# Token-major input and rope tables loaded ahead of the first product weights, and one Strassen sum made by VectorE

## The chip, the cores and the metric

The kernel runs on one core of a Trainium2 chip. The metric is the device time of one execution in microseconds (us), the median of several runs. The core has a matrix engine (TensorE, PE in the profile; its weight loads are PEld), a vector engine (VectorE, DVE), a scalar engine (ScalarE, ACT), a general engine (GpSimd, POOL) and a queue engine (SyncE, SP) that issues most of the transfers. Each takes its instructions in a fixed order that was decided when the program was built. Transfers (DMA) are issued from SP, ACT and POOL and run on 16 shared DMA engines.

## The reference, cut to what matters

Two layers over 512 tokens of width 1024, everything in float32. Each layer normalises its input, multiplies it by a wide input matrix whose columns are queries, keys, values and gates of two attention branches, runs both branches, and projects back.

```python
def rms_norm(x, w, eps):
    return xf * lax.rsqrt(jnp.mean(xf * xf, axis=-1, keepdims=True) + eps) * w

def hybrid_layer(x, layer, ...):
    hdn = rms_norm(x, norm_w, RMS_EPS)
    u = hdn @ w_in                       # 1024 x 10240
    qa, ka, va, za, qb, kb, vb, zb, ga, gb = split_cols(u)
    qa = partial_rope(qa, cos, sin)      # ka, qb, kb as well
    ya = dilated_mixture(qa, ka, va) * silu(za)
    ...                                  # yb: differential attention, silu(zb)
    merged = sigmoid(ga) * (ya @ w_proj_a) + sigmoid(gb) * (yb @ w_proj_b)
    return x + merged @ w_out
# two layers, then a final rms_norm
```

## The kernel before, in words

Every float32 product is made from three float32r products: each operand is split into a high part (a rounded copy) and a low part (the difference), and high x high, high x low and low x high are added up. The row scale of the norm is left out of the products; it is applied to their results. So the products of the first layer can begin before the norm is known, and only what reads their results waits for it.

The weights come as a stream of 512 KB pieces, numbered in the order of `plan()`: `raw0` and `raw1` are the first product chunk (z0, the first gate columns of branch A), `raw2` and `raw3` the second (z1), and eight entries, 4 to 11, the third, "v": the value columns of branch A, a kind "S" chunk. `load_to` (line 86) issues a piece from SP; the pieces of ordinary chunks have three buffers, those of S chunks come from a pool of 29 shared tiles (`blk`). `split` (line 100) makes `whi` (ScalarE, line 103) and `wlo` (VectorE, line 104), each with three buffers, so that a new `whi` waits until TensorE has done with the one three places back.

An S chunk is a 2 x 2 Strassen-Winograd product with seven block products instead of eight. Its weight operands are the quarters 11, 22, 21 and 12 (each in two pieces, p = 0 and 1) and the sums T1 = 12 - 11, T2 = T1 - 22, T3 = 12 - 22 and 21 + T2. `prep_S` (line 122) prepares the 14 operands in the order 11, 21, T1, T2, T3, 22, 21 + T2. T1 and T3 are made by `sum_of` (line 109): ScalarE writes the negative of 11 or 22 (line 112), and a transfer issued by POOL adds quarter 12 from memory to it (line 113, an accumulating transfer). T2 and 21 + T2 are made by VectorE (lines 135 and 137). In the order of TensorE, i.e. of `proj_S`, X takes 11, Z takes 21, Y takes T1, X takes T2, and so on; `S1` to `S4` are the sums on the other side (lines 213 to 238).

The norm's row scale of the first layer is made from a token-major copy of x, four pieces `xt0` to `xt3` (line 837): ScalarE squares and sums them (line 839, eight instructions), VectorE makes a mean (lines 248 and 240), POOL raises it to the power -1/2 (line 241), TensorE turns the result into rows (line 264, the tile `ps_rb`), ScalarE copies that to `rb` (line 269), and POOL multiplies the rope tables `ct` and `st` by it (lines 270 and 271). The evacuations of z0 and z1 on VectorE (line 467) wait for `rb`. `proj_T` (line 274) holds the results of z0 until all this is issued.

The order in each engine's queue is not the order of the code. A scheduler in the framework simulates the engines' times and puts the instructions into their queues by priority and by that simulation; only the first block of ScalarE and VectorE instructions (line 817) keeps its written order. So a change at the start may re-sort instructions elsewhere.

## Time and profile before

| | |
|---|---|
| median of 3 runs | 1385.66 us (1385.55 to 1386.77) |
| the profiled execution | 1387.04 us |
| its span, first to last instruction | 1385.3 us |
| mean granted TensorE clock | 0.994 of full speed |
| TensorE busy | 1351.1 us, 98% |
| VectorE busy | 969.4 us, 70% |
| ScalarE busy | 850.4 us, 61% |
| POOL busy | 324.2 us, 23% |
| moved by DMA | 205.04 MB, mean 148 GB/s |

Busy times are of instructions in flight; matrix products overlap each other, so a busy TensorE shows no idle time while a matrix product of 512 columns starts every 0.23 us. The span begins at the first instruction; the rest of the execution's own time (1.7 us) lies outside it. A gap of an engine is given in brackets in a timeline row, with what ended it.

### The profile page before, as it was taken

The page shows a single profiled execution, that of the slowest core. Times are in us where ns is not written, and L with a number is a line of the kernel's source. Part 1 is how long each engine was busy: PE and PEld are TensorE (multiplying, and loading weights), DVE is VectorE, ACT ScalarE, POOL GpSimd, SP SyncE. Part 2 cuts the span into 40 slices and gives each one's busy share as a digit, 9 for nine tenths or more (in the row PEclk, how much of TensorE's full clock was granted, in tenths as well). Part 3 has the DMA queues.
Part 4 walks back from the last instruction along what each step waited for, and adds up shares of the span by engine and source line. Part 5 has one row for each costly group of instructions (what it writes and reads, how often), then busy time and mean ns, then how long its engine had stood idle before and what let it go on. Part 6 is the DMA issues. An engine that isn't in the chain of part 4 may idle for free.

```text
span 1385.3 us, 19483 instructions
## 1 busy us (share of the span) xinstructions
PE 1351.1 (98%) x6712; PEld 1134.7 (82%) x6712; DVE 969.4 (70%) x1907; ACT 850.4 (61%) x1630; POOL 324.2 (23%) x453
## 2 busy tenths in 40 slices
PE   7799999999999999999999999999999999999996
PEld 6588888888888888888888888878888888888896
DVE  6666787788867786645485677788896678665553
ACT  6655678777555657632566567877756566664332
POOL 0210341333303241110220223232351223211000
PEclk9899999999999999999999999999999999999999
DMA  9654574555735454333586356554565464435231
GB/s 315 211 151 118 157 182 120 141 151 145 190 113 153 137 157 132 123 101 104 182 259 177 88 159 162 146 152 114 153 173 162 122 175 123 144 100 179 94 92 61
DMA packets 82594, 205.04 MB, mean 148 GB/s; under 512 B 11200, under 2 KB 27712, under 8 KB 82496
## 3 DMA queue, kind: packets, MB, share of 16 engines
q1 hardware_dynamic: 45888, 136.67, 30.8%
q0 software_dynamic: 19712, 58.74, 18.6%
q10 hardware_dynamic: 16896, 8.39, 2.0%
q8 instruction: 53, 0.87, 0.3%
q14 instruction: 45, 0.37, 0.1%
HBM read 136.65 MB, written 16.78 MB: 111 GB/s over the span
## 4 chain that ended last, share of the span: by engine, by line
PE 86%; DVE 6%; ACT 3%; DMA 2%; issue 1%; POOL 0%; SPq 0%; DVEq 0%; POOLq 0%; ACTq 0%
PE pj L288 20%; PE pj L289 20%; PE pj L290 20%; PE X L309 2%; PE X L311 2%; PE X L310 2%; DVE wlo L104 1%; DMA xt<-xtok_d 1%; DMA raw<-ws_d 1%; PE Y L310 1%; PE Y L311 1%; PE Y L309 1%; PE pv L309 1%; PE pv L311 1%; PE pv L310 1%
## 5 line engine op out<-in xcount | busy, mean ns | idle before, releaser
L288 PE MATMUL pj<-h,whi 128*128 128x512 f32 x1024 | 405.0, 397 | 7.2 <-DVE whi L823 6.0
L290 PE MATMUL pj<-h,wlo 128*128 128x512 f32 x1024 | 402.9, 396 | 1.1 <-DVE wlo L104 1.1
L289 PE MATMUL pj<-h,whi 128*128 128x512 f32 x1024 | 403.7, 394 | 0.0
L104 DVE TENSOR_TENSOR wlo<-raw,whi 128x1024 fp32r<-128x1024 f32 x207 | 263.2, 1272 | 117.7 <-ACT whi L103 115.8
L103 ACT ACTIVATE whi<-raw 128x1024 fp32r<-128x1024 f32 x207 | 218.6, 1056 | 138.9 <-PE pj L289 99.6
L288 PEld LDWEIGHTS pj<-h,whi 128*128 128x128 f32 x1024 | 193.0, 188 | 46.2 <-issue 6.0
L290 PEld LDWEIGHTS pj<-h,wlo 128*128 128x128 f32 x1024 | 192.9, 188 | 38.9 <-DVE wlo L104 1.6
L289 PEld LDWEIGHTS pj<-h,whi 128*128 128x128 f32 x1024 | 193.0, 189 | 37.3
L718 POOL TENSOR_TENSOR g<-g,pr 128x512 f32<-128x512 f32 x16 | 21.0, 1312 | 151.5 <-ACT g L717 151.5
L104 DVE TENSOR_TENSOR wlo<-T,whi 128x1024 fp32r<-128x1024 f32 x24 | 29.1, 1222 | 15.1 <-ACT whi L103 15.1
L310 PE MATMUL pv<-wlo,mg 128*128 128x256 f32 x128 | 35.7, 283 | 0.0
L311 PE MATMUL pv<-whi,mg 128*128 128x256 f32 x128 | 35.7, 283 | 0.0
L309 PE MATMUL pv<-whi,mg 128*128 128x256 f32 x128 | 35.4, 283 | 0.0
L103 ACT ACTIVATE whi<-T 128x1024 fp32r<-128x1024 f32 x24 | 25.3, 1058 | 12.6 <-PE Z L311 5.9
L726 DVE TENSOR_TENSOR g<-pj,g 128x512 f32<-128x512 f32 x16 | 11.1, 692 | 30.5 <-PE pj L290 30.5
L113 POOL DMA_DIRECT2D T<-ws_d x16 | 14.5, 908 | 68.7 <-ACT T L112 67.6
L715 DVE TENSOR_TENSOR g<-pj,rb 128x512 f32<-128x512 f32 x32 | 21.4, 685 | 10.9 <-PE pj L290 10.6
L730 ACT ACTIVATE mg<-g 128x512 fp32r<-128x512 f32 x16 | 10.1, 631 | 29.5 <-DVE g L727 29.5
L309 PE MATMUL Y<-whi,S 128*128 128x512 f32 x64 | 23.0, 400 | 4.7 <-DVE z(0, 0, 0)_277 L467 4.7
L502 ACT ACT_TABLE_LOAD x21 | 26.9, 1283 | 0.4
L207 POOL TENSOR_TENSOR sq<-sq,sq 128x512 f32<-128x512 f32 x6 | 8.7, 1452 | 75.8 <-ACT sq L203 75.8
L310 PE MATMUL Y<-wlo,S 128*128 128x512 f32 x64 | 25.0, 391 | 0.0
(4002 smaller groups left out, 3304.1 us busy)
## 6 DMA issues: line engine op xcount, KB each, us to landing
raw<-ws_d SPq DMA_DIRECT2D x199, 512.0 KB, 3.9
T<-ws_d POOLq DMA_DIRECT2D x16, 512.0 KB, 8.4
v_dram<-c ACTq DMA_DIRECT2D x24, 256.0 KB, 3.1
pa_dram<-pa SPq DMA_DIRECT2D x16, 256.0 KB, 3.4
pr<-pa_dram SPq DMA_DIRECT2D x16, 256.0 KB, 4.1
xt<-xtok_d SPq DMA_DIRECT2D x4, 512.0 KB, 13.0
v_dram<-v ACTq DMA_DIRECT2D x8, 256.0 KB, 5.0
xr<-x_d SPq DMA_DIRECT2D x8, 256.0 KB, 4.4
```

Source lines behind the costliest of these rows:

```text
L103: nc.scalar.activation(whi[j], src, AF.Copy)
L104: nc.vector.tensor_tensor(wlo[j], src, bits(whi[j]), OP.subtract)
L113: nc.gpsimd.dma_start(out=flat(t), in_=add, accum_op=OP.add)
L288: nc.tensor.matmul(ps, w_h, hb[:, 0], start=(k == 0), stop=False)
L289: nc.tensor.matmul(ps, w_h, hb[:, 1], start=False, stop=False)
L290: nc.tensor.matmul(ps, w_l, hb[:, 0], start=False, stop=(k == 7))
L309: nc.tensor.matmul(ps, hh, w_h, start=first, stop=False, skip_group_check=True)
L310: nc.tensor.matmul(ps, hh, w_l, start=False, stop=False, skip_group_check=True)
L311: nc.tensor.matmul(ps, hl, w_h, start=False, stop=last, skip_group_check=True)
L502: nc.scalar.activation(p, p, AF.Exp, bias=mn[:, i:i + 1], scale=-1.0, accum_out=den[:, i:i + 1])
L715: nc.vector.tensor_tensor(g[:, b], ps, rb, OP.mult)
L718: nc.gpsimd.tensor_tensor(g[:, 0], g[:, 0], st_.pop(("pa", m)), OP.mult)
```

## The change

Three things are written differently. First, the four `xt` pieces and then `ident`, `ct` and `st` are asked for right behind `raw2` and `raw3` in the code, ahead of everything that follows; before, `ident`, `ct` and `st` came after the first products' operands and `xt` after those. Second, `plan()` marks each chunk with a third entry, and the first S chunk of the first layer, `(0, "v", 0)`, has "T1" there: its pieces come in the order 11, 21, 22, 12, quarter 12 as a plain load instead of an accumulating transfer, and its T1 is made by VectorE as 12 - 11 (new line 134). `stage_S`, which made T1 for S chunks, does nothing for this one. T3 is still made by an accumulating transfer, but later, when the third pair of operands is prepared. Third, the other S chunks keep their way (the mark "T1, T3" is given to chunks of another kind, which do not look at it).

```diff
-            need += [n + 3, n + 4, n + 5, n + 6] + [n + 6] * 4 + [n + 8] * 6
+            need += [n + k for k in ((1, 2, 5, 6, 7, 8, 8, 8) if ch[2] else (3, 4, 5, 6, 6, 6, 6, 6))] + [n + 8] * 6
...
     def stage_S(c, p):
 
+        if chunks[c][2]:
+            return
         l0 = first_load[c]
...
-        l0, q, p = first_load[c], quarters, i % 2
+        l0, q, p, here = first_load[c], quarters, i % 2, chunks[c][2]
+
+        def take(name, n):
+            if (c, name, p) not in q:
+                q[c, name, p] = raw.pop(l0 + n + p)
+
+        def minus(name, a, b, of=None):
+            t = q[c, name, p] = of or f4(f"{name}_{c}{p}")
+            nc.vector.tensor_tensor(t, q[c, a, p], q[c, b, p], OP.subtract)
+
         if i < 2:
-            q[c, "22", p] = raw.pop(l0 + 2 + p)
-        elif i < 4:
-            q[c, "21", p] = raw.pop(l0 + 4 + p)
+            take("11", 0)
+        if i < 2 and not here or i in (2, 3):
+            take("22", 2 if not here else 4)
+            if i < 2 or here == "T1":
+                sum_of(c, "T3", p, q[c, "22", p], ws[l0 + 6 + p])
+        if i in (2, 3):
+            take("21", 4 if not here else 2)
+        if i in (4, 5) and here:
+            take("12", 6)
+            minus("T1", "12", "11")
         name = ("11", "21", "T1", "T2", "T3", "22", "21")[i // 2]
         split(j, flat(q[c, name, p]))
-        if i < 2:
-            sum_of(c, "T3", p, q[c, "22", p], ws[l0 + 6 + p])
-        elif i in (4, 5):
-            q[c, "T2", p] = f4(f"T2_{c}{p}")
-            nc.vector.tensor_tensor(q[c, "T2", p], q[c, "T1", p], q[c, "22", p], OP.subtract)
+        if i in (4, 5):
+            minus("T2", "T1", "22")
...
-    load_to(4)
+    xts = []
+    for tb in range(4):
+        if tb % 2 == 0:
+            load_to(3 + tb // 2)
+        xts.append(f4(f"xt{tb}"))
+        nc.sync.dma_start(xts[tb], xtok[tb])
+    nc.sync.dma_start(ident, ident_in)
+    nc.sync.dma_start(ct, rope[0])
+    nc.sync.dma_start(st, rope[1])
...
+            here = "T1" if (layer, *n) == (0, "v", 0) else "T1, T3" if n[0] == "out" else ""
+            chunks.append((kind, (layer, *n), here))
...
-                for kh, p, fh in ((0, 0, 0), (0, 1, 0), (1, 0, 1), (1, 1, 1), (1, 0, 0), (1, 1, 0), (0, 0, 1), (0, 1, 1)):
-                    loads.append((kind if kh >= fh else "add", mat, layer, 512 * kh + 256 * p, 256, f[fh]))
+                q11, q22, q21, q12 = (0, 0), (1, 1), (1, 0), (0, 1)
+                for kh, fh in (q11, q21, q22, q12) if here else (q11, q22, q21, q12):
+                    for p in range(2):
+                        loads.append((kind if here or kh >= fh else "add", mat, layer, 512 * kh + 256 * p, 256, f[fh]))
```

What the scheduler makes of it is shown at three places; the names are tiles with running numbers, `raw` with the number of the weight piece. In the changed code 4 and 5 are quarter 11, 6 and 7 are 21, 8 and 9 are 22, 10 and 11 are 12; before, 6 and 7 are 22 and 8 and 9 are 21.

The first place is the queue of SP at the start. Before, from just behind `raw2`:

```order
L828 DMA ident_92<-ident_in_d 128x128
L829 DMA ct_95<-rope_d 128x512
L830 DMA st_96<-rope_d 128x512
L97 DMA raw4_148<-ws_d 128x1024
L97 DMA raw5_150<-ws_d 128x1024
L97 DMA raw6_152<-ws_d 128x1024
L871 DMA nbt_94<-negb_d 128x1024
L872 DMA sw_in_93<-subln_w_d 128x2
L97 DMA raw3_122<-ws_d 128x1024
L837 DMA xt0_179<-xtok_d 128x1024
L837 DMA xt1_183<-xtok_d 128x1024
L837 DMA xt2_187<-xtok_d 128x1024
```

In the changed kernel, the same queue from the last `xt` piece on; `xt0` to `xt2` stand ahead of it, and `raw2` ahead of those:

```order
L835 DMA xt3_130<-xtok_d 128x1024
L836 DMA ident_92<-ident_in_d 128x128
L837 DMA ct_95<-rope_d 128x512
L838 DMA st_96<-rope_d 128x512
L97 DMA raw4_159<-ws_d 128x1024
L892 DMA nbt_94<-negb_d 128x1024
L893 DMA sw_in_93<-subln_w_d 128x2
L97 DMA raw5_197<-ws_d 128x1024
L97 DMA raw6_229<-ws_d 128x1024
L97 DMA raw3_126<-ws_d 128x1024
L97 DMA raw7_231<-ws_d 128x1024
L97 DMA raw8_233<-ws_d 128x1024
```

All four `xt` pieces moved ahead of the S chunk's pieces; `raw3`, the second half of z1's weights, had eight transfers of 512 KB or less between itself and `raw2` and now has twelve. Quarter 12 comes further down: `raw9`, `raw12`, `raw13`, then `raw10`, `raw22`, `raw11`, and behind it the next S chunk's pieces.

The second place is TensorE, where the row scale is turned (`ps_rb`). Before, it stands inside the first product of the S chunk (X):

```order
L310 MATMUL X2_1_387<-wlo5_359,h0_2_138 128x512
L311 MATMUL X2_1_387<-whi5_358,h0_2_138 128x512
L309 MATMUL X2_0_383<-whi5_358,h0_3_141 128x512
L310 MATMUL X2_0_383<-wlo5_359,h0_3_141 128x512
L264 MATMUL ps_rb_269<-ident_92,rstd_265 128x128 x4
L311 MATMUL X2_0_383<-whi5_358,h0_3_141 128x512
L309 MATMUL X2_1_387<-whi5_358,h0_3_141 128x512
```

In the changed kernel it stands in z1 (`pj1`), just ahead of the first product that reads `whi3`, which is made from `raw3`:

```order
L307 MATMUL pj1_1_336<-h0_2_149,wlo2_194 128x512
L305 MATMUL pj1_1_336<-h0_3_152,whi2_193 128x512
L281 MATMUL ps_rb_263<-ident_92,rstd_259 128x128 x4
L306 MATMUL pj1_1_336<-h0_3_152,whi2_193 128x512
L307 MATMUL pj1_1_336<-h0_3_152,wlo2_194 128x512
L305 MATMUL pj1_0_281<-h0_4_161,whi3_225 128x512
L306 MATMUL pj1_0_281<-h0_4_161,whi3_225 128x512
L305 MATMUL pj1_1_336<-h0_4_161,whi3_225 128x512
L306 MATMUL pj1_1_336<-h0_4_161,whi3_225 128x512
L326 MATMUL X2_0_378<-whi4_275,h0_0_139 128x512
L326 MATMUL X2_1_382<-whi4_275,h0_0_139 128x512
L307 MATMUL pj1_0_281<-h0_4_161,wlo3_226 128x512
```

The four turns moved 46 matrix products forward. The number of matrix products and their work are the same.

The third place is VectorE from the first `wlo` of quarter 21 to the first `wlo` of T1 (`wlo8`). Before:

```order
L104 TENSOR_TENSOR wlo6_380<-raw8_236,whi6_379 128x1024
L135 TENSOR_TENSOR T2_20_421<-T1_20_203,raw6_152 128x1024
L236 TENSOR_TENSOR S3_00_437<-S3f00_323,S3_00_437 128x512
L236 TENSOR_TENSOR S3_01_440<-S3f01_325,S3_01_440 128x512
L137 TENSOR_TENSOR raw8_236<-raw8_236,T2_20_421 128x1024
L236 TENSOR_TENSOR S4_00_443<-S4f00_327,S4_00_443 128x512
L236 TENSOR_TENSOR S4_01_446<-S4f01_329,S4_01_446 128x512
L467 TENSOR_TENSOR z(0, 0, 0)_277<-pj0_0_206,rb_97 128x512
L467 TENSOR_TENSOR z(0, 0, 0)_277<-pj0_1_210,rb_97 128x512
L467 TENSOR_TENSOR z(0, 0, 1)_343<-pj1_0_290,rb_97 128x512
L467 TENSOR_TENSOR z(0, 0, 1)_343<-pj1_1_345,rb_97 128x512
L135 TENSOR_TENSOR T2_21_453<-T1_21_238,raw7_201 128x1024
```

In the changed kernel:

```order
L104 TENSOR_TENSOR wlo6_373<-raw6_229,whi6_372 128x1024
L134 TENSOR_TENSOR T1_20_415<-raw10_353,raw4_159 128x1024
L104 TENSOR_TENSOR wlo7_396<-raw7_231,whi7_395 128x1024
L134 TENSOR_TENSOR T2_20_421<-T1_20_415,raw8_233 128x1024
L253 TENSOR_TENSOR S3_00_437<-S3f00_314,S3_00_437 128x512
L253 TENSOR_TENSOR S3_01_440<-S3f01_316,S3_01_440 128x512
L134 TENSOR_TENSOR T1_21_449<-raw11_376,raw5_197 128x1024
L253 TENSOR_TENSOR S4_00_443<-S4f00_318,S4_00_443 128x512
L253 TENSOR_TENSOR S4_01_446<-S4f01_320,S4_01_446 128x512
L154 TENSOR_TENSOR raw6_229<-raw6_229,T2_20_421 128x1024
L104 TENSOR_TENSOR wlo8_418<-T1_20_415,whi8_417 128x1024
```

The evacuations of z0 and z1 left this stretch for an earlier place, two subtractions for T1 came into it, and `wlo7` no longer stands behind the evacuations. Four of POOL's accumulating transfers stood before its multiplications of the rope tables; now two stand behind them, and two are gone. From there on the queues read alike up to the second layer, where the engines' orders differ between the attention head 3 of branch A and head 2 of branch B.

## Rows read from the trace of the kernel before

**Rows 1.** Busy time by stretch: us, length, engines' busy time (instructions), TensorE clock, DMA share, GB/s.

```profile
0.00:58.00 58.00, 40.55 (x151) 30.64 (x152) 41.15 (x59) 35.30 (x54) 9.35 (x13) 0.91 0.83 282
66.00:1375.00 1309.00, 1302.51 (x6528) 1097.46 (x6526) 922.87 (x1841) 807.61 (x1566) 314.27 (x439) 1.00 0.50 142
```

**Rows 2.** The chain that ended last, its first 60 us: start, us, what.

```profile
18.53 16.48 DMA xt<-xtok_d
...
36.85 1.05 POOL rstd L241
...
48.75 1.20 DVE z(0, 0, 0)_277 L467 x2
```

**Rows 3.** Timeline of TensorE: start, us, instruction [idle before it, what ended that].

```profile
24.75 0.39 PE L288 MATMUL pj<-h,whi 128*128 128x512 f32 x1
...
27.42 0.50 PE L290 MATMUL pj<-h,wlo 128*128 128x512 f32 x1 [1.15 <-DVE wlo L104]
...
37.95 0.65 PE L264 MATMUL ps_rb<-ident,rstd 128*128 128x128 f32 x4 [1.61 <-POOL rstd L241]
...
40.69 0.50 PE L309 MATMUL Z<-whi,h 128*128 128x512 f32 x1 [1.16 <-ACT whi L103]
41.95 0.50 PE L310 MATMUL Z<-wlo,h 128*128 128x512 f32 x1 [0.76 <-DVE wlo L104]
...
50.09 1.30 PE L309 MATMUL Y<-whi,S 128*128 128x512 f32 x2 [4.67 <-DVE z(0, 0, 0)_277 L467]
53.46 0.80 PE L310 MATMUL Z<-wlo,h 128*128 128x512 f32 x1 [2.07 <-DVE wlo L104]
...
57.90 0.47 PE L310 MATMUL Y<-wlo,S 128*128 128x512 f32 x1
...
63.47 0.39 PE L310 MATMUL X<-wlo,S 128*128 128x512 f32 x1
```

**Rows 4.** Timeline of ScalarE, copies that waited for `raw4` and for `raw6`.

```profile
17.25 1.06 ACT L112 ACTIVATE T<-raw 128x1024 f32<-128x1024 f32 x1 [1.74 <-DMA raw<-ws_d]
...
19.81 1.06 ACT L112 ACTIVATE T<-raw 128x1024 f32<-128x1024 f32 x1 [0.21 <-DMA raw<-ws_d]
```

**Rows 5.** Groups of DVE in 0 to 60 us: busy us, mean ns of one.

```profile
L104 DVE TENSOR_TENSOR wlo<-raw,whi 128x1024 fp32r<-128x1024 f32 x7 | 8.5, 1219 | 5.6 <-ACT whi L103 5.6
...
L236 DVE TENSOR_TENSOR S<-S3f,S 128x512 fp32r<-128x512 f32 x2 | 2.4, 1236 | 0.0
...
L236 DVE TENSOR_TENSOR S<-S4f,S 128x512 fp32r<-128x512 f32 x2 | 1.3, 679 | 0.0
```

**Rows 6.** Groups of ACT in 0 to 60 us.

```profile
L103 ACT ACTIVATE whi<-raw 128x1024 fp32r<-128x1024 f32 x7 | 7.3, 1053 | 1.5 <-PE X L311 1.5
...
L839 ACT ACTIVATE xt<-xt 128x512 f32<-128x512 f32 x8 | 5.0, 622 | 5.3 <-DMA xt<-xtok_d 5.3
```

**Rows 7.** Busy time by stretch, without and with POOL's accumulating transfers.

```profile
14.50:22.00 7.50, 7.49 (x33) 5.91 (x32) 7.50 (x14) 5.31 (x7) 2.79 (x3) 1.00 1.03 406
22.00:34.00 12.00, 10.85 (x48) 8.65 (x47) 7.72 (x12) 7.71 (x17) 0.03 (x1) 1.00 1.06 286
```

**Rows 8.** Busy time by stretch around the 4.67 us gap of TensorE.

```profile
47.00:47.50 0.50, 0.00 (x0) 0.00 (x0) 0.50 (x2) 0.48 (x2) 0.00 (x0) 1.00 0.84 328
47.50:48.00 0.50, 0.00 (x0) 0.00 (x0) 0.50 (x2) 0.50 (x1) 0.00 (x0) 0.83 0.51 188
...
53.40:57.50 4.10, 4.04 (x10) 3.18 (x11) 4.05 (x5) 1.06 (x1) 0.43 (x1) 0.50 0.41 128
...
58.00:58.50 0.50, 0.50 (x4) 0.42 (x3) 0.36 (x1) 0.36 (x1) 0.00 (x0) 0.93 0.00 0
```

**Rows 9.** Waits of TensorE from 910 to 1060 us: us in total, times, longest.

```profile
PE t((1, 0, 3), 1)2_8417 L520 <- DVE pt L522: 1.2, 1, 1.2
PE s(1, 1, 1)12_9836 L499 <- DVE mn(1, 1, 1)1_9792 L501: 1.1, 1, 1.1
```

**Rows 10.** Busy time of the stretch whose order differs in the second layer.

```profile
911.00:1055.00 144.00, 141.18 (x715) 118.31 (x714) 120.12 (x271) 103.05 (x225) 50.81 (x79) 1.00 0.59 156
```

More of the change, by code (lines that the diff above doesn't have):

```diff
@@ L122, in prep_S @@
     def prep_S(j, c, i):
-        l0, q, p = first_load[c], quarters, i % 2
-        if i < 2:
-            q[c, "22", p] = raw.pop(l0 + 2 + p)
-        elif i < 4:
-            q[c, "21", p] = raw.pop(l0 + 4 + p)
+        l0, q, p, here = first_load[c], quarters, i % 2, chunks[c][2]
[5 more added lines that the diff above has]
+            nc.vector.tensor_tensor(t, q[c, a, p], q[c, b, p], OP.subtract)
+        if i < 2:
+            take("11", 0)
[8 more added lines that the diff above has]
+            minus("T1", "12", "11")
         name = ("11", "21", "T1", "T2", "T3", "22", "21")[i // 2]
         split(j, flat(q[c, name, p]))
-        if i < 2:
-            sum_of(c, "T3", p, q[c, "22", p], ws[l0 + 6 + p])
-        elif i in (4, 5):
-            q[c, "T2", p] = f4(f"T2_{c}{p}")
-            nc.vector.tensor_tensor(q[c, "T2", p], q[c, "T1", p], q[c, "22", p], OP.subtract)
+        if i in (4, 5):
+            minus("T2", "T1", "22")
+        elif i in (6, 7) and here == "T1, T3":
+            minus("T3", "12", "22", q[c, "12", p])
         elif i in (8, 9):
@@ L827, in trunk_kernel @@
         raw.pop(0)
-    nc.sync.dma_start(ident, ident_in)
-    nc.sync.dma_start(ct, rope[0])
-    nc.sync.dma_start(st, rope[1])
     for m in range(NB):
@@ L835, in trunk_kernel @@
     for tb in range(4):
-        xt = f4(f"xt{tb}")
-        nc.sync.dma_start(xt, xtok[tb])
+        xt = xts[tb]
         for n in range(2):
@@ L937, in plan @@
             kind = "S" if n[0] == "v" else "T"
-            chunks.append((kind, (layer, *n)))
+            here = "T1" if (layer, *n) == (0, "v", 0) else "T1, T3" if n[0] == "out" else ""
+            chunks.append((kind, (layer, *n), here))
             mat = n[0] if n[0] in ("pa", "pb", "out") else "in"
```

## The prediction

> **What bounds the kernel now.** I read the busy time by stretch first. From 66 us to 1375 us TensorE is busy for 1302.5 of 1309 us at full clock: nothing outside it can gain there. In the first 58 us it is busy for 40.6 us, at a mean clock of 0.91 [rows 1]. So what the change can give lies in these 58 us, and what it gives there reaches the end of the span undiminished, because every later product stands behind on an engine that has no slack.
>
> Then the chain that ended last says what the beginning waits for: 16.5 us of it are the last `xt` transfer, then the power on POOL, then VectorE's evacuations of z0 and z1 [rows 2]. The timeline of TensorE gives the gaps: 1.15 us in z1, 1.61 us for the row scale at `ps_rb`, 1.16 and 0.76 us for the operands of Z, 4.67 us with the evacuations named, 2.07 us for `wlo7`, which stands behind the same evacuations [rows 3]. They add up to 11.4 us. In the longest gap the granted clock goes from 1.00 to 0.50, and it is back at full only at 58 us [rows 8]: the products from 53.46 us to 57.90 us, ten of them, start 0.44 us apart, where the 24 from 57.90 us to 63.47 us start 0.23 us apart [rows 3]. That is 10 x 0.21 = 2.1 us more.
>
> **Part one, the order of the loads.** Transfers of SP land in the order of the queue: `raw4`, `raw5` and `raw6` stand one behind another, and the first and the last end waits of ScalarE at 17.25 and 19.81 us, 1.28 us per 512 KB [rows 4]. I take the changed queue with this step from `raw4`'s place. Four `xt` pieces ahead of it make 17.25 + 4 x 1.28 = 22.4 us for `raw4`; `nbt`, `raw5`, `raw6` and `raw3` follow, so `raw3` lands at 22.4 + 4 x 1.28 = 27.5 us. This step holds only while POOL's accumulating transfers are absent: all queues move 406 GB/s without them and 286 GB/s in the stretch with them [rows 7]; in the changed kernel they come after `raw8`, so `raw3` is ahead of them all.
>
> The row scale gains. The last `xt` lands at 22.4 - 1.28 (`raw4`) - 1.4 (`ident`, `ct`, `st`, 576 KB) = 19.7 us. Two squares of 0.62 us follow [rows 6], VectorE's two small instructions with two sums between them, and 1.05 us on POOL [rows 2]: about 24 us. `ps_rb` stands behind 70 products, which now as before end at about 24.5 us, so it waits for nothing. The 1.61 us gap goes.
>
> The second half of z1 loses. TensorE has its last product before `whi3` two places behind the turns, so it is done at 24.75 + 0.4 for the turns, with the drain 25.3 us [rows 3]. `raw3` at 27.5 us and 1.05 us for `whi3` [rows 6] let it go on at 28.7 us. A new gap of 3.4 us stands where 1.15 us stood.
>
> `rb` stands behind `whi3` and `whi4` on ScalarE, so it comes at 28.6 + 1.05 + 0.6 = 30.2 us, ahead of everything in the S chunk that waited for it before. The evacuations of z0 need only that; those of z1 wait for its products, and nobody waits for them but VectorE's own queue. POOL's multiplications of the rope tables then run beside VectorE's `wlo4`, the evacuations of z0 and `wlo5`; the splits of S3, which had such neighbours, took 1.24 us where those of S4 took 0.68 us [rows 5]. If all four double, that is 3.8 us more, and `wlo5` would be done at about 37 us, when X asks for it (28.7 + 38 x 0.23 = 37.4 us). I take nothing, and 0 to 1 us in the range; a gain is excluded, as it was not slowed here before.
>
> **Part two, T1 on VectorE.** It removes two accumulating transfers and two negated copies of ScalarE, and adds two loads on SP and two subtractions of 1.22 us on VectorE, the duration of a `wlo` of the same size [rows 5]. The load of piece 11 is the last one that matters: after `raw3` come `raw7`, 8, 9, 12, 13, 10, 22 and 11, eight times 1.28 us, 37.8 us. The two accumulating transfers for T3 are issued behind the rope tables, so no sooner than `rb` at 30.2 us and probably at 33 us. If the last three loads then take 1.28 x 406 / 286 = 1.8 us each [rows 7], the piece lands at 39.4 us; in the chain's 16.5 us [rows 2] seven pieces landed beside such transfers (`raw6`, `nbt`, `raw3`, four `xt`), 2.4 us each, and by that it lands at 41 us. By the Trainium skill, page "DMA: Bandwidth & Descriptors", section "Queues, rings and completion order", an engine takes turns between the queues that have work for it; by an even split the last three loads would take twice 1.28 us each, 41.6 us, and the 2.4 us of the chain agree with that.
>
> **Where the next bound is.** With TensorE going from 28.7 us, the 72 products to the end of Z take 72 x 0.23 = 16.6 us: 45.3 us. Then Y needs `wlo8`, and that is a chain on VectorE. `whi6` waits for the buffer of `whi3`, which z1's last product frees at 28.7 + 26 x 0.23 = 34.7 us; ScalarE then has a Silu in its way, so `whi6` is there at about 36.5 us. From there VectorE has eleven instructions one after another: `wlo6`, T1, `wlo7`, T2, two splits of S3, T1, two splits of S4, 21 + T2, `wlo8`. Seven of 1.17 us (1.22 us each, less the overlap of neighbours) and four of 0.64 us, from rows of 1219 and 679 ns [rows 5], are 10.8 us: 47.3 us. So Y's first product with a low part starts at 47.3 us, 2 us behind the end of Z less the 0.9 us of four early products; 22 products later, at 47.3 + 22 x 0.23 = 52.4 us, comes X's first low product of T2. From that product on both orders are the same up to the second layer, and before it started at 63.47 us [rows 3]. **11.1 us are gained if the clock holds.** T1's second piece may land as late as 42 us at no cost, since its subtraction stands behind the splits of S3.
>
> **The clock.** The new gap is 3.4 us. Gaps of 1.61 us left the clock at 1.00; in the one of 4.67 us, which began at 50.09 - 4.67 = 45.4 us, it fell between 47.5 and 48 us, some 2.3 us in [rows 3, 8]. I take it that it falls again. TensorE then goes on from 28.7 us at half its speed for about as long as the last time, 4.4 us, and loses 2.1 us. Z ends at 47.4 us; the chain on VectorE shifts by about 1 us since z1 ends later, and the four early products end at about 49.2 us, when `wlo8` is already there. The gain is 11.1 - 1.9 = 9.2 us. The Trainium skill, page "TensorE: Matmul & The Clock Gate", section "HAM oscillation", speaks against this change: waits for loads between groups of products make the clock fall back and the next group start cold. The fall in the trace agrees with it; by that page the price would be half of the time at the low clock, 2.2 us, which is the measured one.
>
> Against the profiled execution, 1387.04 us, this gives 1377.8 us. It stands 1.4 us above the median of the runs, 1385.66 us, and the span itself is near that median, so I take the gain from the median: **1376.5 us**.
>
> **What is left at nothing.** The two squares and evacuations have moved, not grown. The next S chunk's T1 is still accumulated; its copies come later in ScalarE's queue than `whi10`, but its products are over 40 us further on. The second layer's changed order covers 144 us, in which TensorE now waits 1.2 and 1.1 us [rows 9]. I take no difference; from both sides it is a gain of 2.3 us to a loss of some such waits more, 3 us.
>
> **The rivals.**
> - *The clock holds.* The gap could be shorter than I make it, or the clock's fall could come too late. For it: it fell only 2.3 us into the long gap, and the new one is over 1.1 us later. Against it: TensorE had been working at full clock and still lost it within 3 us. It gives 1385.7 - 11.1 = 1374.5 us.
> - *The wait moves to T1.* Pieces 10 and 11 stand behind `raw12` and `raw13` and about `raw22`, whose buffers are freed by VectorE only; a load that is blocked there blocks those behind it. For it: `raw22` waits for `wlo3`, and VectorE has nearly no slack from 36 to 54 us. Against it: `wlo3` is due at 29.9 us, eight transfers ahead. If piece 11 came 4 us later than it may, 46 us, Y would start 4 us later: 9.2 - 4 = 5.2 us, 1380.5 us.
> - *The change gives it back at z1.* If the loads ran at 286 GB/s from the start, the 5.3 MB between `raw2` (14.5 us) and `raw3` would take 18.6 us: 33.1 us, 5.6 us later, 1382 us. Against it: what made that rate was POOL's transfers, and they are gone from this place [rows 7].
> - *Slower, by the second layer.* Its order is re-sorted from head 3 of branch A to head 2 of branch B. VectorE is busy there for 120 of 144 us [rows 10], and every wait of a turn for VectorE's copy costs 1.2 us [rows 9]; the stretch has a dozen half-heads with three groups of turns each. From eight such waits the gain is gone, from ten the kernel is slower by over 0.2%; twelve give 1376.5 + 14.4 = 1391 us. Against it: the same heads in the order before have only two waits, and the products between them are the same.
>
> **How the numbers follow.** The forecast 0.52, with 1374.8 to 1378.5 us of its own; the clock holds 0.22; the wait moves to T1 0.13; given back at z1 0.08; slower 0.05. The first three lie between 1372.5 us (the clock holds, and the second layer loses its 2.3 us of waits) and 1381 us; the other two are mostly outside. That is the range. A difference of under 0.2%, 2.8 us, can hardly be told from none here; so faster means under 1382.9 us: the first three and half of the fourth, 0.91; the same 0.05; slower 0.04.
>
> **What would show it.** In the profile after, ScalarE's first square should start at 16 us and the last end before 21 us, `ps_rb` run near 25 us without a wait, and TensorE have one gap of 3 to 4 us before the first product with `whi3`, ended by ScalarE. The clock row just behind it decides between the first two cases. Z should follow X without a gap, the evacuations no longer end any wait of TensorE, and X's first low product of T2 start at 52 to 55 us. A second gap ahead of Y, ended by VectorE's T1 or `wlo8`, of more than 3 us would make the forecast wrong, and so would waits of more than 6 us in all between 900 and 1050 us, or `raw3` landing after 30 us.

## The result, and the profile after

The changed kernel takes **1375.88 us** (median of 4 runs, 1375.41 to 1377.29) beside 1385.69 us of the kernel before in the same job: ratio 0.9927, 95% interval 0.9913 to 0.9941, so it is 0.7% faster. The forecast was 1376.5 us. The profiled execution took 1376.04 us, its span 1374.3 us.

Busy time by stretch, in the columns of [rows 1]:

```profile
0.00:47.00 47.00, 36.73 (x150) 29.12 (x150) 37.27 (x58) 33.46 (x52) 8.16 (x10) 1.00 0.95 331
24.00:54.00 30.00, 26.88 (x120) 21.50 (x119) 27.96 (x35) 21.37 (x27) 7.18 (x5) 1.00 0.90 278
900.00:1044.00 144.00, 141.84 (x720) 119.05 (x719) 119.91 (x273) 104.84 (x225) 52.67 (x79) 1.00 0.59 156
```

TensorE issues about as many products in 47 us as it did in 58 us before (150 and 151), and the granted clock is 1.00 from 24 to 54 us, where [rows 8] show it at 0.50. The third row answers to [rows 10]; it begins 11 us sooner, because the work of that stretch now stands some 10 us sooner.

The chain of waits, its two longest transfers of the start:

```profile
9.23 10.46 DMA xt<-xtok_d
20.15 7.51 DMA raw<-ws_d
```

The last `xt` is there at 19.7 us (before, 35.0 us [rows 2]) and `raw3` at 27.7 us. The evacuations of z0 are no longer in the chain of this stretch. TensorE's timeline, to be laid beside [rows 3]:

```profile
15.61 0.50 PE L305 MATMUL pj<-h,whi 128*128 128x512 f32 x1 [1.26 <-ACT whi L103]
...
25.73 0.60 PE L281 MATMUL ps_rb<-ident,rstd 128*128 128x128 f32 x4
...
28.85 0.50 PE L305 MATMUL pj<-h,whi 128*128 128x512 f32 x1 [2.06 <-ACT whi L103]
...
45.12 0.39 PE L328 MATMUL Z<-whi,h 128*128 128x512 f32 x1
45.35 0.61 PE L326 MATMUL Y<-whi,S 128*128 128x512 f32 x2
47.03 0.73 PE L326 MATMUL X<-whi,S 128*128 128x512 f32 x2 [1.06 <-ACT whi L103]
47.60 0.40 PE L327 MATMUL Y<-wlo,S 128*128 128x512 f32 x1
...
52.60 0.39 PE L327 MATMUL X<-wlo,S 128*128 128x512 f32 x1
...
58.58 0.50 PE L326 MATMUL X<-whi,S 128*128 128x512 f32 x1 [0.82 <-ACT c L372]
```

The reader is to see four gaps, 1.26, 2.06, 1.06 and 0.82 us, together 5.2 us where six made 11.4 us; `ps_rb` without a wait; and X's first low product of T2 at 52.60 us instead of 63.47 us, 10.87 us sooner. VectorE's timeline around the chain that the forecast counted:

```profile
36.44 1.23 DVE L104 TENSOR_TENSOR wlo<-raw,whi 128x1024 fp32r<-128x1024 f32 x1 [0.62 <-ACT whi L103]
...
42.19 1.22 DVE L134 TENSOR_TENSOR T<-raw,raw 128x1024 f32<-128x1024 f32 x1
43.33 1.29 DVE L253 TENSOR_TENSOR S<-S4f,S 128x512 fp32r<-128x512 f32 x2
44.53 1.22 DVE L154 TENSOR_TENSOR raw<-raw,T 128x1024 f32<-128x1024 f32 x1
45.67 1.22 DVE L104 TENSOR_TENSOR wlo<-T,whi 128x1024 fp32r<-128x1024 f32 x1
```

From `wlo6` at 36.44 us to the end of `wlo8` at 46.9 us it doesn't wait, and T1's second piece (42.19 us) waits for no load. But `wlo8` is not what ends the gap of 1.06 us. In TensorE's order X's first two products of T2 stand between Y's first two products and Y's low ones, and they wait for `whi10`, whose buffer Z's last product frees; `wlo8` is there 0.7 us before its first reader at 47.60 us. Then ScalarE, with `whi10` and with its queue just before the gap at 58.58 us:

```profile
45.92 1.06 ACT L103 ACTIVATE whi<-T 128x1024 fp32r<-128x1024 f32 x1 [1.33 <-PE Z L328]
...
55.11 1.05 ACT L112 ACTIVATE T<-raw 128x1024 f32<-128x1024 f32 x1
56.05 1.04 ACT L103 ACTIVATE whi<-T 128x1024 fp32r<-128x1024 f32 x1
57.01 1.04 ACT L112 ACTIVATE T<-raw 128x1024 f32<-128x1024 f32 x1
57.95 1.06 ACT L372 ACTIVATE c<-X 128x512 f32<-128x512 f32 x2
```

Two negated copies for the next chunk's T1 stand ahead of the copy of X that TensorE waits for. The chain of waits reaches that copy from VectorE's `wlo9` through ScalarE's queue:

```profile
48.02 1.15 DVE wlo L104
49.19 0.92 ACT T L112
...
58.05 0.49 ACT c L372
```

### The profile page after: what moved, and what is told of

It reads as the page before. It is cut to its first block, busy times and chain, and to the rows that moved or that the text cites. A ratio compares the mean times of both kernels' runs of the same rounds, so it can differ in the third digit from the quotient of the medians.

```text
span 1374.3 us, 19490 instructions
## 1 busy us (share of the span) xinstructions
PE 1347.1 (98%) x6712; PEld 1133.2 (82%) x6712; DVE 967.0 (70%) x1909; ACT 849.3 (62%) x1628; POOL 325.6 (24%) x451
## 4 chain that ended last, share of the span: by engine, by line
PE 88%; DVE 4%; ACT 3%; DMA 2%; issue 1%; SPq 0%; POOL 0%; ACTq 0%; POOLq 0%; DVEq 0%
PE pj L305 21%; PE pj L306 21%; PE pj L307 21%; PE X L326 2%; PE X L327 2%; PE X L328 2%; DVE wlo L104 1%; PE pv L326 1%; PE pv L328 1%; PE pv L327 1%; PE Y L327 1%; PE Y L326 1%; PE Y L328 1%; DMA xt<-xtok_d 1%; ACT whi L103 1%
## 5 line engine op out<-in xcount | busy, mean ns | idle before, releaser
L743 DVE TENSOR_TENSOR g<-pj,g 128x512 f32<-128x512 f32 x16 | 11.1, 692 | 30.5 <-PE pj L307 30.5
L326 PE MATMUL X<-whi,S 128*128 128x512 f32 x64 | 24.2, 398 | 1.9 <-ACT whi L103 1.1
L327 PE MATMUL X<-wlo,S 128*128 128x512 f32 x64 | 24.9, 390 | 0.0
```

Of the source, the lines that this page charges most:

```text
L326: nc.tensor.matmul(ps, hh, w_h, start=first, stop=False, skip_group_check=True)
L327: nc.tensor.matmul(ps, hh, w_l, start=False, stop=False, skip_group_check=True)
L743: nc.vector.tensor_tensor(g[:, 1], ps, g[:, 1], OP.mult)
```

## The experiments

What had to be explained: which part gives the gain, why the clock held, and what sets the time now. My theory became this: behind the two loads, VectorE's chain to `wlo9` and then ScalarE's queue near 58 us set the pace, so an early gap is worth only what it passes on to them. The rival: each gap of TensorE is worth its length plus the clock. Each job had its own runs of the kernel before (medians 1386.17, 1387.28 and 1386.42 us); times within a job are compared first.

**1. The order of the loads alone** (all of T1 accumulated, as before):

```diff
-            here = "T1" if (layer, *n) == (0, "v", 0) else "T1, T3" if n[0] == "out" else ""
+            here = ""
```

> Part one alone: xt, ident, ct and st early, but T1 and T3 of the first S chunk still made by accumulating transfers. Theory A (the row scale was what blocked TensorE, the order of the loads is the gain): the evacuations of z0 and z1 end no wait any more, and 7 us or more are gained, 1379 us or less. Theory B (the accumulating transfers were the root, since the loads beside them took 2.4 us instead of 1.28 us per 512 KB): raw3 now stands behind four more loads and beside four accumulating transfers, lands at 31 to 34 us instead of 27.7 us, TensorE gets a gap of 5 us or more there with the clock falling, and the gain is 2 to 6 us, 1380 to 1384 us.

1379.76 us, ratio 0.9951 (0.9939 to 0.9964): 6.4 us gained. TensorE's timeline and a stretch of clock:

```profile
29.42 0.50 PE L305 MATMUL pj<-h,whi 128*128 128x512 f32 x1 [3.81 <-ACT whi L103]
32.79 0.80 PE L307 MATMUL pj<-h,wlo 128*128 128x512 f32 x1 [1.24 <-DVE wlo L104]
```

```profile
31.00:37.00 6.00, 4.76 (x12) 3.38 (x11) 5.75 (x5) 4.68 (x7) 0.65 (x1) 0.50 1.06 275
```

Here the long gap stands that the forecast drew for the changed kernel, and the clock falls, though not in the gap: it falls in the slice from 30 to 31 us (0.72), when TensorE has worked again for a microsecond. The rate is 275 GB/s while the accumulating transfers for T1 and T3 run. The result lies between the two theories: under 7 us gained, but a gap of under 5 us.

**2. T1 by VectorE alone** (the loads in the order of before, `ident`, the tables and `xt` back in their old places):

```diff
-    xts = []
-    for tb in range(4):
-        if tb % 2 == 0:
-            load_to(3 + tb // 2)
-        xts.append(f4(f"xt{tb}"))
-        nc.sync.dma_start(xts[tb], xtok[tb])
...
+    load_to(4)
```

> Part two alone: T1 of the first S chunk by VectorE from a plain load, xt, ident, ct and st where they were before. Theory A: the row scale is late as before, the evacuations still end a wait of several us, under 4 us are gained, 1382 us or more. Theory B: with no accumulating transfer beside them the last xt piece lands at about 25 us instead of 35 us, raw3 at 20 us so that z1 has no gap, the row scale is turned at about 33 us inside X without a long wait, and 9 to 13 us are gained, 1373 to 1377 us: part one was not needed, and by the 2 to 3 us of the raw3 gap it even costs.

1377.48 us, ratio 0.9937 (0.9924 to 0.9951): 8.7 us gained, just short of theory B's 9 us, with no gap in z1 or at `ps_rb`. The wait has gone to `wlo9`, with the clock behind it:

```profile
49.74 0.79 PE L327 MATMUL Y<-wlo,S 128*128 128x512 f32 x1 [3.53 <-DVE wlo L104]
```

```profile
49.00:55.00 6.00, 5.25 (x12) 4.12 (x13) 4.09 (x4) 2.93 (x4) 0.90 (x2) 0.50 0.55 122
```

The parts don't add up: 6.4 and 8.7 us alone, 9.8 us together. Either removes the wait for the evacuations.

**3. `raw3` early**, in a buffer of its own, so that `whi3`'s gap goes:

```diff
-            if loads[j][0] == "S":
+            if loads[j][0] == "S" or j == 3:
```

> The changed kernel with raw3 in a tile of the shared pool instead of the third weight buffer, so that its load needs no wait and goes out between xt1 and xt2. If the gap of 2.06 us before the first product with whi3 is on the path in full, it goes, and 2 to 3 us more are gained, 1373 to 1374 us. If VectorE's chain from whi6 to wlo8 sets the time of Y (my sum), TensorE arrives at Y earlier and waits there longer: 0 to 1 us, 1375 to 1376 us.

1379.76 us (1379.36 to 1380.37), ratio 0.9952 (0.9940 to 0.9965): 3.9 us *slower* than the changed kernel's median, though a gap of 2 us is gone; neither case of the expectation had a loss. TensorE, VectorE and the clock:

```profile
51.21 0.79 PE L327 MATMUL Y<-wlo,S 128*128 128x512 f32 x1 [3.54 <-DVE wlo L104]
```

```profile
37.41 1.23 DVE L104 TENSOR_TENSOR wlo<-raw,whi 128x1024 fp32r<-128x1024 f32 x1 [1.60 <-ACT whi L103]
...
41.79 1.23 DVE L134 TENSOR_TENSOR T<-raw,raw 128x1024 f32<-128x1024 f32 x1 [0.76 <-DMA raw<-ws_d]
...
49.94 2.35 DVE L104 TENSOR_TENSOR wlo<-T,whi 128x1024 fp32r<-128x1024 f32 x2
```

```profile
51.00:56.00 5.00, 4.79 (x11) 3.80 (x12) 3.57 (x4) 1.77 (x3) 0.86 (x1) 0.50 0.88 219
```

TensorE comes sooner to operands that VectorE hasn't made: waits of 1.20 and 3.54 us at Y, the second long enough for the clock. VectorE itself waited 1.60 us for `whi6` and 0.76 us for a load. The scheduler also put the splits of S3 and S4 between `wlo8` and `wlo9`.

**4. 256 KB more ahead of `raw2`** (one extra load, its data unused), meant to make one gap of 3.3 us before `whi3`.

```diff
+    nc.sync.dma_start(f4("more")[:, 0], xtok[0, :, 0])
```

> The changed kernel with one more load of 256 KB ahead of raw2; the scheduler also puts raw7 ahead of raw3. raw2 lands 0.64 us later, raw3 1.9 us later (29.7 us), so the gap before whi3's first product is 3.3 us, about the one that I forecast, with the gap of 1.26 us at whi2 growing to 1.9 us. If a single gap of that size makes the clock fall, as I forecast, the granted clock is 0.50 for some us behind it and the time is 2 to 4 us above the changed kernel's, 1378 to 1380 us. If it takes a longer gap, the clock stays at 1.00 and the time is 0.5 to 2 us above, 1376.4 to 1378 us.

1375.56 us, ratio 0.9925 (0.9912 to 0.9937): no difference to the changed kernel. It missed its purpose, for the delay fell on `whi2` too: gaps of 2.47 us there and 1.71 us at `whi3`. Behind the first the clock fell for some 3 us, behind the second it was 1.00:

```profile
16.58 0.73 PE L305 MATMUL pj<-h,whi 128*128 128x512 f32 x1 [2.47 <-ACT whi L103]
```

```profile
17.00:20.00 3.00, 3.00 (x8) 2.32 (x8) 2.97 (x6) 3.00 (x11) 0.00 (x0) 0.50 1.03 392
```

What a longer early gap costs, it can't say: TensorE's order of Z and Y was re-sorted as well, and only one gap of 0.51 us is left behind these two. The three executions with a mean granted clock of 0.997 or 0.998 took 1375.11 to 1375.56 us; the profiled one, at 0.996, took 1376.77 us, and the fifth, at 0.994, 1377.22 us.

**5. The splits of S3 and S4 earlier**, by eight steps of V:

```diff
-        run(v[:12] + [(0, lambda: h_split(layer, ("S3", "S4")))] + v[12:])
+        q = 4 if layer == 0 else 12
+        run(v[:q] + [(0, lambda: h_split(layer, ("S3", "S4")))] + v[q:])
```

> The changed kernel, with the splits of S3 and S4 (four copies of ScalarE, four subtractions of VectorE of 0.6 us) written eight steps of V earlier in the first layer. In VectorE's order they move from the chain whi6 to wlo8 to in front of it, between the two evacuations of z1. Theory A (VectorE's chain sets the start of Y): wlo8 is done 2 us sooner than 46.9 us, so the gap of 1.06 us ahead of Y goes and X's first low product of T2 starts near 51.5 us instead of 52.6; the time is 0.9 to 1.3 us below the changed kernel's, about 1375 us beside a before of 1386. Theory B (the last load, raw11, sets it: in the kernel with raw3 early T1's second piece waited for it until 41.8 us): T1's second piece waits, wlo8 is at most 0.5 us sooner, and the time stays within 0.4 us. Theory C (ScalarE's four earlier copies delay whi4 or whi6): a gap appears between 32 and 38 us and the time is 1 us or more longer.

1375.45 us (1375.10 to 1376.26), ratio 0.9915 (0.9901 to 0.9928): not told apart from the changed kernel. Its rows show what came of it. VectorE:

```profile
43.05 1.22 DVE L104 TENSOR_TENSOR wlo<-T,whi 128x1024 fp32r<-128x1024 f32 x1
```

TensorE and the clock:

```profile
28.20 0.50 PE L305 MATMUL pj<-h,whi 128*128 128x512 f32 x1 [2.07 <-ACT whi L103]
...
46.72 0.39 PE L327 MATMUL Y<-wlo,S 128*128 128x512 f32 x1
...
49.44 0.61 PE L326 MATMUL X<-whi,S 128*128 128x512 f32 x2
```

```profile
29.00:32.00 3.00, 3.00 (x8) 2.32 (x8) 3.00 (x5) 3.00 (x6) 2.34 (x2) 0.50 1.02 407
```

`wlo8` is done at 44.3 us, 2.6 us sooner, and Y's gap is gone, as theory A said. But X's first two products of T2 now stand behind 14 of Y's products (49.44 us) and no longer ahead of the low ones, so TensorE comes to them when `whi10` is there; this run can't tell which of the two ended the gap. Behind the gap of 2.07 us the clock fell, for some 3 us. X's first low product of T2 came at 52.16 us, 0.4 us sooner, not 1.1. The three executions at a mean clock of 0.997 took 1375.10 to 1375.45 us, the two at 0.996, the profiled one among them, 1376.23 and 1376.26 us.

**6. Both: `raw3` early and the splits earlier** (the edits of 3 and 5), and **7.** with T3 by VectorE too:

```diff
-            here = "T1" if (layer, *n) == (0, "v", 0) else "T1, T3" if n[0] == "out" else ""
+            here = "T1, T3" if (layer, *n) == (0, "v", 0) else "T1, T3" if n[0] == "out" else ""
```

> The kernel with raw3 early (1379.8 us), with the splits of S3 and S4 written eight steps of V earlier as well. Theory A (raw3 early lost because TensorE arrived sooner at operands that VectorE still had to make, in one gap of 3.54 us in which the clock fell): with 2.6 us of splits out of that chain wlo9 is done near 49 us instead of 52.3, the gap at Y shrinks to 2 us or less, the clock stays at 1.00 from 28 to 56 us, and the time falls by 3 to 5 us, to 1375 to 1376.5 us, level with the changed kernel or a little below. Theory B (raw3's own buffer, taken from the other pool, costs time elsewhere): the gap at Y shrinks, but the time stays at 1379 to 1380 us, with new waits after 60 us.

> As the kernel before in this list, and T3 of the first chunk also made by VectorE, so no accumulating transfer is issued before 50 us. Theory A (VectorE's chain sets Y): one more subtraction of 1.14 us stands ahead of wlo8 and two ahead of wlo9, so Y's waits grow by 1 to 2 us in all against the kernel with raw3 and the splits early, and the time is 0 to 3 us longer. Theory B (the transfers set it: the DMA rate falls to 120 to 215 GB/s between 36 and 43 us while POOL's two accumulating transfers run): raw10 and raw11 land 2 us sooner or more, near 39 us, the rate stays above 350 GB/s until they are there, and the time is 0.5 to 1.5 us shorter.

1376.15 us (0.9922, 0.9910 to 0.9935) and 1375.78 us (0.9918, 0.9904 to 0.9932). Of the 3.9 us that `raw3` early had cost, 3.6 us came back when 2.6 us of splits left VectorE's chain, with `raw3`'s buffer as it was: its loss was that chain and the clock behind it, not the buffer. Between 6 and 7 no difference can be told; T1's second piece waited for no load in either, so the transfers weren't the limit. In 6, TensorE's and VectorE's timelines say what is left:

```profile
39.54 0.50 PE L327 MATMUL Z<-wlo,h 128*128 128x512 f32 x1 [1.28 <-DVE wlo L104]
49.82 0.50 PE L327 MATMUL Y<-wlo,S 128*128 128x512 f32 x1 [1.13 <-DVE wlo L104]
```

```profile
33.46 1.29 DVE L253 TENSOR_TENSOR S<-S3f,S 128x512 fp32r<-128x512 f32 x2 [2.13 <-ACT S L252]
```

**8. 256 KB more behind the rope tables** (the line of experiment 4 put there; `raw7` to `raw9` then also go ahead of `raw3`).

> The changed kernel with one more load of 256 KB behind the rope tables; by the scheduler's answer raw7, raw8 and raw9 also go ahead of raw3, so raw3 lands 4 x 1.28 + 0.64 us less the place of nbt's row, near 33 us instead of 27.7. Theory A (the forecast's step on the clock: one gap of 3.4 us or more makes it fall, two of 1.3 and 2.1 us do not): one gap of about 7 us ahead of the first product with whi3, in which the granted clock goes to 0.50 and is back at 1.00 some 4 to 5 us after work begins again; the time is the changed kernel's plus 5 us for the later load plus 1 to 2 us for the clock, 1382 to 1383 us. Theory B (the clock held in the changed kernel because of where the gap stands, early in the program, not because of its length): the clock stays at 1.00, and the time is 1380.5 to 1381 us.

1383.34 us, ratio 0.9971 (0.9960 to 0.9982). TensorE and the clock:

```profile
35.29 0.79 PE L305 MATMUL pj<-h,whi 128*128 128x512 f32 x1 [8.59 <-ACT whi L103]
```

```profile
32.00:38.00 6.00, 2.71 (x6) 2.15 (x7) 2.73 (x3) 5.99 (x7) 0.88 (x1) 0.50 1.06 326
```

The gap is longer than expected and 6.5 us longer than in the changed kernel; it is the only one behind the start besides 0.92 us at `whi2`. TensorE's last product ends 6.7 us later, so in sum nearly all of it is paid. Theory B, that an early place protects the clock, is refuted.

**9 and 10. The changed kernel again**, for two more profiles.

> The changed kernel itself once more, for a second profile, since the kernel with the splits early lost the clock behind a gap of 2.07 us before whi3 and the changed kernel kept it behind one of 2.06 us. Theory A (it was chance: the gap's length between about 2 and 2.5 us does not settle whether the clock falls, and what stood before it moves with the moment at which the clock came up at the start): the clock behind whi3's gap may be 0.50 or 1.00 in this execution; the gap ahead of Y shrinks by about as much as Z comes later if it falls, so the time stays 1375.5 to 1376.5 us either way. Theory B (two shorter gaps, 1.26 us at whi2 and 2.06 us at whi3, never cost the clock): both gaps stand as before within 0.3 us and the clock is 1.00 from 24 to 54 us.

> The changed kernel a third time, for one more profile. Theory A: the gap at whi2 is anything from 0 to 1.3 us, longer where the clock came up sooner after the first product, and the clock behind whi3's gap is 0.50 in some execution. Theory B: the same gaps and the clock at 1.00.

1375.50 us (1374.84 to 1376.95, 5 runs; ratio 0.9920, 0.9906 to 0.9934) and 1376.02 us (one run). In the first the gap of `whi3` is 2.04 us and the clock holds; in the second it is 2.01 us and the clock falls. TensorE of the first:

```profile
29.00 0.50 PE L305 MATMUL pj<-h,whi 128*128 128x512 f32 x1 [2.04 <-ACT whi L103]
...
47.16 0.72 PE L326 MATMUL X<-whi,S 128*128 128x512 f32 x2 [1.06 <-ACT whi L103]
...
52.75 0.39 PE L327 MATMUL X<-wlo,S 128*128 128x512 f32 x1
```

TensorE and the clock of the second:

```profile
28.17 0.80 PE L305 MATMUL pj<-h,whi 128*128 128x512 f32 x1 [2.01 <-ACT whi L103]
...
47.87 0.72 PE L326 MATMUL X<-whi,S 128*128 128x512 f32 x2 [1.06 <-ACT whi L103]
...
53.46 0.39 PE L327 MATMUL X<-wlo,S 128*128 128x512 f32 x1
```

```profile
29.00:31.00 2.00, 2.00 (x6) 1.52 (x6) 2.00 (x3) 2.00 (x4) 1.37 (x1) 0.50 1.04 416
```

On the clock theory A holds: same kernel, same gap, either clock. Its second half failed: the gap ahead of X was to shrink by as much as Z came later, and it is 1.06 us in all three profiles: X follows the start of Z's last product by 1.91 us in the result's profile (45.12 us) and by 1.90 us here (45.97 us). What the fall costs shows only when it is counted from the same product, for `whi3` came 0.7 to 0.8 us sooner in this execution than in the other two. From its first product to X's first low product of T2 it is 25.29 us here and 23.75 us in both others: 1.54 us. Later waits hide a part of that. The wait for `c` near 58 us is 0.82 us in the result's profile, 0.19 us in experiment 9 and absent here, and to the end of TensorE's last product the fall leaves 0.66 us against the one and 1.34 us against the other. That the ends themselves lie at 1363.25, 1362.72 and 1363.23 us is due to the sooner start.

**11. `raw3` early and the splits ahead of all of V** (experiment 6 with the first line below), and **12.** that with `raw2` loaded ahead of the last blocks of x:

```diff
-        q = 4 if layer == 0 else 12
+        q = 0 if layer == 0 else 12
...
         if i == 1:
             load_to(2)
+        if i == 2:
+            load_to(3)
```

> raw3 early, and the splits of S3 and S4 written twelve steps of V earlier, in front of V. In the profile of the kernel that wrote them eight steps earlier VectorE waited 2.13 us at 33.46 us for ScalarE's copies of S3, which stood behind rb; here they stand before rb, and the subtractions in VectorE's order before wlo4. Theory A (VectorE's chain still sets Z and Y in that kernel): the gap of 1.28 us at wlo7 and that of 1.13 us at wlo9 shrink to 0.5 us or less in sum, and the time is 1 to 2 us below the changed kernel's in this job, about 1374.3 us. Theory B (the gaps only move: to whi2, which is 0.7 to 1.8 us, or to ScalarE's c copies near 58 us): gaps before 60 us sum to as much as before, and the time stays within 0.5 us of the changed kernel's.

> The same, and raw2 loaded ahead of the last two blocks of x, so that whi2 comes 1.28 us sooner and the last h blocks 1.28 us later. Theory A (whi2's gap is worth its length): no gap at whi2, and 0.7 to 1.3 us less than the kernel beside it. Theory B (what TensorE does not wait for at whi2 it waits for at h6 or at raw3's or raw4's products, since all loads up to 28 us are one queue at 400 GB/s): the time is the same within 0.4 us, with a gap of 0.5 us or more at another place before 30 us.

Number 11 takes **1373.86 us** (1373.77 to 1375.02), ratio 0.9909 (0.9896 to 0.9923), 1.6 us under the changed kernel's 1375.50 us in the same job; the ranges of the runs overlap by 0.2 us, so it is the best of all, by little. Its waits of TensorE to 66 us, and the middle stretch:

```profile
PE pj L305 <- DVE whi L848: 6.4, 1, 6.4
PE pj L305 <- ACT whi L103: 1.7, 1, 1.7
PE Y L327 <- DVE wlo L104: 0.4, 1, 0.4
```

```profile
24.00:54.00 30.00, 29.56 (x132) 24.16 (x132) 28.80 (x37) 24.67 (x32) 7.71 (x7) 1.00 0.94 311
```

Behind the start only 2.1 us of gaps are left, where the changed kernel had 5.2 us, and in 24 to 54 us TensorE issues 132 products instead of 120. So the two edits together pay, by theory A's size (1 to 2 us). How much of it is `raw3`'s is not shown, since the splits ahead of V were not run without it.

Number 12 takes 1375.12 us (0.9917, 0.9904 to 0.9931): `whi2`'s gap falls from 1.68 to 0.76 us, and new ones of 0.85 and 0.79 us stand before Z and in Y, beside one of 0.50 us in Y (0.44 us in number 11). Neither theory held: what TensorE doesn't wait for at `whi2` it waits for elsewhere, as B said, but at 36 and 45 us and not before 30 us, and the median is 1.3 us longer, with 0.2 us of overlap between the ranges.

## Why the prediction was right

*Loads.* Right. `raw3` at 27.7 us (forecast 27.5), the last `xt` at 19.7 us (19.7), the power done at 24.0 us (about 24), `ps_rb` without a wait, at 25.73 us instead of 24.5 to 25, because of the gap at `whi2`. `rb` was done at 30.2 us (30.2). Nothing was seen of VectorE being slowed beside POOL's tables: the two evacuations of z0 and the `wlo` behind them took 1.28 and 1.22 us.

*The chain to Y.* Its times are right to a few tenths, its last wait is not. Z's last product started at 45.12 us (end forecast 45.3), `wlo6` at 36.44 us (36.5), `wlo8` was done at 46.9 us (47.3), X's first low product of T2 came at 52.60 us (52.4). 10.87 us are gained there (11.1). But "Then Y needs `wlo8`" left out `whi10`: of the "four early products" two wait for it, it waits for Z's last product, and it came 0.1 us after `wlo8`. That both came at the same time is luck. Piece 11 was no wait; in experiment 3 a subtraction waited for it until 41.8 us, just past the forecast's 39.4 to 41.6 us. The Trainium skill, page "DMA: Bandwidth & Descriptors", section "Queues, rings and completion order", has an engine take turns between queues that have work. By an even split, an estimate from that rule, the piece would land at 41.6 us; that row, of a kernel with another order of loads, is close to it.

*The new gap.* Right in sum, wrong in form. I had one of 3.4 us; there were two, 1.26 and 2.06 us, 3.32 in all. The first four products of z1 stand six rows earlier in TensorE's order than before, ahead of most of `h4`'s, and wait for `whi2`. That was in the order of the changed kernel and I overlooked it.

*The clock: the step that failed.* "TensorE then goes on from 28.7 us at half its speed for about as long as the last time, 4.4 us, and loses 2.1 us." Of three profiles of this kernel two kept 1.00 and one fell to 0.50, for about 3 us; all four executions of the result have the mean clock of the two that kept it, 0.997. Where it fell, it cost 1.54 us at X, and 0.66 or 1.34 us of that at the end of the program, as experiment 10 shows. The forecast's price of 1.9 us is near, but not by its own sum: Z's end at 47.4 us and four products of 0.23 us make 48.3 us; the 49.2 us come out only at 0.44 us each, at a clock that by the same text is back by then. With 48.3 us the price is 1.0 us and the forecast 1375.6 us. What stood there in truth was the wait for `whi10`. In experiments 1 to 3, with gaps of 3.5 us and more, the clock did fall, for 6 to 7 us; so the rule I used fits gaps of that size, and I had the gap's size from a sum. The page "TensorE: Matmul & The Clock Gate" of the Trainium skill, section "HAM oscillation", says that waits for loads between groups of products set the clock back; experiments 1, 4, 5, 8 and 10 agree, while behind the waits of 2.06 and 2.04 us in the other two profiles of the changed kernel it held.

*"From that product on both orders are the same."* Nearly. ScalarE's order wasn't: the negated copies of the next chunk's T1, which I let pass at no cost, stand ahead of `c`, 0.82 us. The first layer ends 10.0 us sooner instead of 10.9. In the second layer the first wait of [rows 9] is still there, 1.16 us at 903.48 us; that of 1.1 us is gone, and a new one of 0.67 us stands at 1033.17 us. The gain at TensorE's end is 10.9 us again. I had taken no difference there, within a bound of 2.3 us gained.

*From the profile to the runs.* The gain is 11.0 us between the two profiled executions and 9.8 us between the medians, since the profiled execution of before ran 1.4 us above its median and that of after 0.2 us above. With the clock held, as in that profile, the forecast would have been 1374.5 us, the rival's, 1.4 us too low; the clock's term of 1.9 us happened to cancel most of that. That the forecast is 0.6 us off is partly luck.

*The rivals.* The wait didn't move to T1, and z1 gave nothing back. "The clock holds" was met by two profiles of three. The second layer went the other way from the rival for slower. The lower end of the range is 1372.2 us by its own terms, not 1372.5.

*What sets the time now.* With `raw3` early it is VectorE's chain, and that is shown: experiments 3, 6 and 11 differ in the code only in where the splits of S3 and S4 are written, and 6 and 11 are 3.6 and 5.9 us faster than 3. For the changed kernel itself it is argued, from the chain of waits of its profile; experiment 5, which takes the splits out of VectorE's chain alone, gained nothing that can be told apart. That an early gap costs nothing is not shown: experiment 10 has it hidden in part, experiment 8 hardly at all. In experiments 4 to 7 and 12 every execution with a mean clock of 0.996 or less took longer than every one of the same kernel with 0.997 or more, by about 0.8 us or more, so the fall is not free. What stays open: why the clock fell behind one gap of 2 us and not behind another.

## What to carry to other kernels

When a wait is removed, follow the chain of the engine that feeds the next operand to its end: removing a further gap in front of a busy feeder (experiment 3) only collects the waiting in one place, where it can cost the clock too. Two changes that each end the same wait don't add up, and the second one is worth what the next feeder leaves. Before pricing a gap, read the waiting engine's order in the changed kernel from the start, since a scheduler may have divided it, and note every operand of the products behind it: the one forgotten here came last. To price something from two profiles of one kernel, count from the same instruction, since the start differs by more than the effect.

## What the runs showed of the hardware

- Gaps of TensorE of almost one length, and the granted clock after them: 2.04 and 2.06 us, 1.00; 2.01 and 2.07 us, 0.50 for about 3 us, and so after 2.47 us (experiment 4). After every gap of 3.5 us or more (3.53, 3.54, 3.81, 8.59, and 4.67 before) it was 0.50, for 6 to 7 us in the four of these experiments; in experiment 1 it held for the first microsecond of work.
- In the gap of 8.59 us the clock fell in the slice from 31 to 32 us, about 5 us after TensorE's last product; in [rows 8] it was some 2.3 us into the gap.
- Where the clock fell behind a gap of 2.01 us, 1.54 us were lost up to X's first low product of T2.
- With POOL's four accumulating transfers under way the rate was 275 GB/s (experiment 1, 31 to 37 us). In the changed kernel it was 410 GB/s from 28.85 to 33 us, before POOL issued its two, and 190 GB/s from 37 to 42 us, behind them.
